# The moving weights of the q, k and v sums read column by column from two runs of 256 columns

## The chip, the cores and the metric

The kernel runs on one core of a Trainium2 chip. The metric is the time of one execution on the device, in microseconds. The kernel before takes 2652.43 us, the median of three runs (2650.87 to 2653.06).

## What is computed

The reference is a trunk of two layers over 256 tokens of width 2048, in float32. A layer is a mixer (two attentions side by side, with gates) and a gated feed-forward part with a convolution. What the change touches is the first step of the mixer: the products of the normalised input with the columns of `w_in` that give queries, keys and values.

```python
h = rmsnorm(x, norm_mix[l]) * (1.0 + sc_a) + sh_a
qa, ka, va, qb, kb, vb, ga, gb = split_cols(h @ w_in[l])
qa = rotary_partial(rmsnorm(qa.reshape(B, S, HA, HEAD_DIM), qn_a[l]), pos)
ka = rotary_partial(rmsnorm(ka.reshape(B, S, GA, HEAD_DIM), kn_a[l]), pos)
va = va.reshape(B, S, GA, HEAD_DIM)
ya = window_attention(qa, ka, va, sink_a[l]) @ w_proj_a[l]
qb = rmsnorm(qb.reshape(B, S, HB, HEAD_DIM), qn_b[l])
kb = rmsnorm(kb.reshape(B, S, HB, HEAD_DIM), kn_b[l])
vb = vb.reshape(B, S, HB, HEAD_DIM)
yb = neighbourhood_attention(qb, kb, vb, rel_bias_b[l]) @ w_proj_b[l]
```

The columns of q, k and v number 4608, in nine groups of 512; a head has 128 of them.

## The kernel before

**Numbers.** Every large product runs in a reduced float32 form. An operand is kept as two halves, a rounded high part and what is left of it, and a product is the sum of three matmuls: high by high, high by low, low by high. Weights come from memory in units of 16 blocks of 128 by 128 (tile `w`, 1 MB each) in the order of use. ScalarE rounds a unit (L346) and VectorE subtracts to get the low half (L347), into tiles `hl` that hold the high and the low half of eight blocks each, 1024 columns per half.

**Two ways round.** In most products the weights are stationary and 256 tokens are the moving operand; that is `feature_block`, L363 to L365, with the tile `ps`. In the sums for q, k and v it is the other way: `tokens` (L417 to L434) keeps 128 tokens of the input `h` stationary and moves four blocks of weights, 512 neighbouring columns of `hl`, past it, so that tokens lie on partitions of the result. Each call has two PSUM tiles `ps_t` of 512 columns, one for each half of the tokens, and for every chunk `kc` of the input six matmuls, L427 to L429 for each half. There are 1728 of them in all.

**Stages.** Layer 0 goes over its nine groups three times, each time with as many of the 16 chunks as are normalised by then (`K_ENDS`): the first part leaves its sums in the packs in SBUF through copies on ScalarE (L967), the second and third add to them on VectorE (L969). Layer 1 has one part with all 16 chunks, and its readers work on PSUM directly: copies of v on ScalarE (L980), and in `qk_rows` a square per head and token half on ScalarE (L599, tile `qsq`) and the product with the root on VectorE (L609, tile `qn`). In layer 0 those two read the packs. Group 0 holds k and v of the first attention, 256 columns each; groups 4 and 7 are v of the second; the others are four heads of q or k.

**Order.** The program's order is set by the loops; background jobs (the products for the modulation on VectorE at L246, attention heads, copies of 32 by 32 blocks on GpSimd) are handed out once per unit of 16 blocks by `tick`. Weights are split a unit or two ahead. PSUM has four buffers for sums, so that a call's readers work while the next call's matmuls run.

Of the kernel before, what the change touches and what calls it, by code (L numbers as in the profile page):

```python
# [11 lines left out]
AF = mybir.ActivationFunctionType  # L12
ALU = mybir.AluOpType
AX = mybir.AxisListType

P = 128
# [4 lines left out]
HEAD = 128  # L21
HA, GA, HB = 8, 2, 8
# [121 lines left out]
def encoder(ctx: ExitStack, tc: tile.TileContext, a: dict, out: bass.AP):  # L144
    nc = tc.nc
# [46 lines left out]
    def place(tag, n, dt, name):  # L192
        return sp.tile([P, n, S], dt, name=name, tag=tag)
# [113 lines left out]
    def later(n, fn):  # L307

        if n == 0:
            fn()  # L310
        else:
            bg.defer(lambda: later(n - 1, fn))
# [54 lines left out]
    class Stream:  # L367
# [49 lines left out]
        def tokens(self, h, kcs):  # L417

            pss = [mm.tile([P, 512], F32, name=f"ps{self.l}_{self.u}_t{t}", tag="mm") for t in range(2)]
            for kc in kcs:  # L420
                for _ in range(4):
                    hl, j = self.next_block()
                j -= 3
                hi, lo = hl[:, 0, j * P : (j + 4) * P], hl[:, 1, j * P : (j + 4) * P]
                for t, ps in enumerate(pss):
                    xh, xl = (h[kc][:, i, t * P : (t + 1) * P] for i in range(2))
                    nc.tensor.matmul(ps[:], xh, hi, start=kc == kcs[0], stop=False)  # L427
                    nc.tensor.matmul(ps[:], xh, lo, start=False, stop=False)  # L428
                    nc.tensor.matmul(ps[:], xl, hi, start=False, stop=kc == kcs[-1])  # L429
                if self.l == 0 and self.u == 1 and self.at == 4:  # L430
                    warm(WARM_ROW)
                if self.at == UB:
                    self.tick()
            return pss  # L434

    def split(dst, src, scale=None, held=False):

# [152 lines left out]

    def qk_rows(pss, heads, rot, gain, dst, then, moved=False, pinned=False):

        cols = 0
        n = heads * HEAD
        ss = sm.tile([P, 8], F32, name="qss", tag="qss")
        for t, ps in enumerate(pss):
            for i in range(heads):
                sq = at.tile([P, HEAD], F32, name="qsq", tag="qsq", bufs=1)
                nc.scalar.activation(  # L599
                    out=sq[:], in_=ps[:, cols + i * HEAD : cols + (i + 1) * HEAD], func=AF.Square,  # L600
                    accum_out=ss[:, t * heads + i : t * heads + i + 1],
                )
        rs = sm.tile([P, 8], F32, name="qrs", tag="qrs")
        rsqrt(rs[:, : 2 * heads], ss[:, : 2 * heads], HEAD, 2 * heads)
        def norm():
            qn = at.tile([P, 8 * HEAD], F32, name="qn", tag="qn", bufs=1)[:, : 2 * n]
            qn = qn.rearrange("p (t h d) -> p t h d", t=2, d=HEAD)
            for t, ps in enumerate(pss):
                product = nc.vector.tensor_tensor(  # L609
                    out=qn[:, t],  # L610
                    in0=ps[:, cols : cols + n].rearrange("p (h d) -> p h d", d=HEAD),
                    in1=rs[:, t * heads : (t + 1) * heads].unsqueeze(2).broadcast_to([P, heads, HEAD]),
                    op=ALU.mult,
                )
                if pinned:
                    tc.keep_in_program_order(product)
            if rot is not None:
                x1, x2 = qn[:, :, :, :HALF], qn[:, :, :, HALF:ROT]
                tab = [rot[:, i].unsqueeze(2).broadcast_to([P, 2, heads, HALF]) for i in range(4)]
                tm = []  # L620
                for i in range(2):
                    z = ev.tile([P, S], F32, name=f"rt{i}", tag="z")
                    z = z[:].rearrange("p (i t h d) -> p i t h d", i=2, t=2, h=4)
                    tm += [z[:, 0, :, :heads], z[:, 1, :, :heads]]
                for i, src in enumerate((x1, x2, x2, x1)):
                    nc.vector.tensor_tensor(out=tm[i], in0=src, in1=tab[i], op=ALU.mult)
                nc.vector.tensor_tensor(out=x1, in0=tm[0], in1=tm[1], op=ALU.subtract)
                nc.vector.tensor_tensor(out=x2, in0=tm[2], in1=tm[3], op=ALU.add)
            bg.defer(lambda: turn(qn))

        def turn(qn):
            if moved:
                nc.vector.transpose(out=qn, in_=qn)
                moved_blocks(dst.rearrange("p h (t s) -> p h t s", t=2), qn.rearrange("p t h d -> p h t d"))

                def scaled():
                    tc.keep_in_program_order(nc.scalar.activation(out=dst, in_=dst, func=AF.Identity, scale=gain))
                    then()

                later(QK_STEPS, scaled)  # L640
                return
            for t in range(2):
                ps = ax.tile([P, 4, P], F32, name="qtp", tag="ax")
                for h in range(heads):
                    nc.tensor.transpose(ps[:, h], qn[:, t, h], ident[:])
                scaled = nc.scalar.activation(
                    out=dst[:, :, t * P : (t + 1) * P], in_=ps[:, :heads], func=AF.Identity, scale=gain
                )
                if pinned:
                    tc.keep_in_program_order(scaled)  # L650
            then()

        bg.defer(lambda: bg.defer(lambda: bg.defer(norm)))
# [116 lines left out]
    with tc.high_priority():  # L770
# [13 lines left out]
        for i in range(KC // 4):  # L784
            sq = place(("y0", "y1", "y2", "a")[i], 12 if i == 3 else 4, F32, f"sq_in{i}")
# [16 lines left out]
        ps = ax.tile([P, 2], F32, name="ss_in", tag="ss", bufs=1)  # L802
# [34 lines left out]
    for l in range(L):  # L837
        st = Stream(l) if l == 0 else nxt
        mod = mods.get(l)
        if l == 0:  # L840
            h = led("h0_0", K_ENDS[0][0][1])
# [13 lines left out]
        if l:  # L855
# [13 lines left out]
            h = bare.h  # L869
# [6 lines left out]
        ready, heads = [0], [0]  # L876
# [78 lines left out]
        for pi, (groups, gates) in enumerate(parts):  # L955
            last = pi == len(parts) - 1
            for g, part in enumerate(groups):
                have_h(part)
                pss = st.tokens(h, part)
                if pi == max(0, len(parts) - 2) and g == 0:  # L960
                    gains, sink, cw, rots = small(l)
                dst = packs[g // 3][:, 4 * (g % 3) : 4 * (g % 3) + 4]
                rows = dst.rearrange("p (t a) s -> p t (a s)", t=2)
                if not last or pi > 0:
                    for t, ps in enumerate(pss):
                        if pi == 0:
                            nc.scalar.copy(rows[:, t], ps[:])  # L967
                        else:
                            nc.vector.tensor_tensor(out=rows[:, t], in0=ps[:], in1=rows[:, t], op=ALU.add)  # L969
                    pss = [rows[:, t] for t in range(2)]  # L970
                if not last:
                    continue

                def turned(g=g):
                    ready[0] = g + 1

                vcol = {0: GA * HEAD, 4: 0, 7: 0}.get(g)
                if vcol is not None and pi == 0:
                    for t in range(2):
                        nc.scalar.copy(rows[:, t, vcol:], pss[t][:, vcol:])  # L980
                if g == 0:
                    qk_rows(pss, GA, rots[1], gains[:, 1:2], kTa, turned, g in MOVED_QK[l], l == 1)
                elif g < 3:
                    qk_rows(pss, 4, rots[0], gains[:, 0:1], dst, turned, g in MOVED_QK[l], l == 1)
                elif vcol is None:
                    qk_rows(pss, 4, None, gains[:, 3:4] if g in (3, 6) else gains[:, 2:3], dst, turned, g in MOVED_QK[l], l == 1)
                else:
                    turned()
                if g == (1 if l in EARLY else 2):
                    bg.add(job, ATT[l])  # L990


            have_h(gates)
            for mo in range(BARE[0] if l else 0, KC):

                def gate_a(ps):
                    src = ps
                    if pi > 0:
                        nc.vector.tensor_tensor(out=ya[:, mo], in0=ps, in1=ya[:, mo], op=ALU.add)  # L999
                        src = ya[:, mo]  # L1000
                    if last:
                        half_tanh(ya[:, mo], src)
                    elif pi == 0:
                        nc.scalar.copy(ya[:, mo], ps)

                st.features([hs[k] for k in gates], [gate_a])
# [14 lines left out]
        for tag in ("y0", "y1", "y2"):  # L1021
            t = place(tag, 4, F32, f"gb{l}_{tag}")
            gb += [t[:, i] for i in range(4)]
        for i in range(2):
            t = paired(F32, f"gb{l}_{i}")
# [207 lines left out]
```

## Time and profile before

| | |
|---|---|
| median of three runs | 2652.43 us |
| span of the profiled execution | 2649.9 us, on one core |
| instructions in the trace | 50997 |
| memory read | 695.06 MB, 263 GB/s over the span |
| reads of the weight units | 463 of 1024 KB, 4.9 us each from issue to landing |

The span runs from the first to the last instruction of the profiled execution; its own time isn't given apart from it, and 2.5 us lie between the span and the median. In the lines of groups, a name such as `ps_t<-hl,h` gives the tile written and the tiles read; then come the shapes, the count, the busy time in us and the mean duration of one in ns, and the idle time just before them. A matmul's record lasts from its start to the end of its last result, and records of matmuls that follow each other overlap. In the view of waits, a row gives the total in us, how often, and the longest.

### The profile page before, as it was taken

What the parts mean: (1) busy time and instruction counts of PE and PEld (TensorE: products, weight loads), DVE (VectorE), ACT (ScalarE), POOL (GpSimd) and SP (SyncE); (2) the same over time, 40 slices, a digit from 0 to 9 for tenths busy, and PEclk for the clock granted to TensorE, in tenths of its full rate; (3) what the DMA queues carried; (4) which work ended last, traced back from release to release, by engine and by line L of the source; (5) the groups of instructions that cost most, each with busy time, mean ns of one, the idle gap of its engine ahead of it and who ended that gap; (6) DMA issues with size and microseconds to landing.
All of it is one profiled execution on the core that took longest, in us unless ns stands there. A gap on an engine that the chain in (4) does not pass through costs nothing.

```text
span 2649.9 us, 50997 instructions
## 1 busy us (share of the span) xinstructions
PE 2638.7 (100%) x21164; PEld 2553.2 (96%) x21164; DVE 2121.3 (80%) x2979; ACT 1407.4 (53%) x2280; POOL 235.7 (9%) x345
## 2 busy tenths in 40 slices
PE   9999999999999999999999999999999999999999
PEld 7888899999999999999998889999999999999999
DVE  8898998997987888788886778868888876655664
ACT  5445865456653554355554666555575445544553
POOL 0001100000000000000002558620000000000000
PEclk9999999999999999999999999999999999999999
DMA  9988789885777877777766666677757775555554
GB/s 366 344 332 300 264 299 353 325 305 210 281 293 284 298 290 295 291 287 291 297 226 239 252 223 244 251 266 273 275 183 273 287 271 192 193 197 195 195 191 143
DMA packets 102185, 700.45 MB, mean 264 GB/s; under 512 B 12865, under 2 KB 15169, under 8 KB 18113
## 3 DMA queue, kind: packets, MB, share of 16 engines
q1 hardware_dynamic: 101954, 697.20, 71.4%
q8 instruction: 165, 2.70, 0.4%
q14 instruction: 66, 0.54, 0.1%
HBM read 695.06 MB, written 2.10 MB: 263 GB/s over the span
## 4 chain that ended last, share of the span: by engine, by line
PE 90%; DVE 6%; ACT 1%; issue 1%; DMA 1%; POOL 0%; DVEq 0%; ACTq 0%
PE ps L363 25%; PE ps L365 25%; PE ps L364 25%; PE ps_t L429 4%; PE ps_t L428 4%; PE ps_t L427 4%; DVE hl L347 2%; DVE aw L246 2%; PE sc L674 1%; DMA aw<-in_aw 1%; PE po L712 1%; ACT hl L346 1%; PE warm L462 0%; PE tp L704 0%; PE cb L776 0%
## 5 line engine op out<-in xcount | busy, mean ns | idle before, releaser
L347 DVE TENSOR_TENSOR hl<-w,hl 128x1024 fp32r<-128x1024 f32 x928 | 1132.7, 1226 | 341.6 <-ACT hl L346 337.1
L346 ACT CAST hl<-w 128x1024 fp32r<-128x1024 f32 x928 | 970.5, 1049 | 752.1 <-PE ps L365 522.7
L363 PE MATMUL ps<-h,hl 128*128 128x256 f32 x3328 | 922.1, 277 | 1.3 <-DVE ya L999 0.6
L364 PE MATMUL ps<-h,hl 128*128 128x256 f32 x3328 | 919.2, 276 | 0.0
L365 PE MATMUL ps<-h,hl 128*128 128x256 f32 x3328 | 919.0, 276 | 0.0
L363 PEld LDWEIGHTS ps<-h,hl 128*128 128x128 f32 x3328 | 624.6, 188 | 2.3 <-DVE ya L999 0.8
L364 PEld LDWEIGHTS ps<-h,hl 128*128 128x128 f32 x3328 | 624.7, 188 | 0.4 <-DVE h L522 0.2
L365 PEld LDWEIGHTS ps<-h,hl 128*128 128x128 f32 x3328 | 624.2, 188 | 0.0
L246 DVE CUSTOM_DVE_ANT_0 aw<-aw,cact,ab 128x2048 f32<-128x2048 f32 x189 | 443.7, 2348 | 9.1 <-DMA aw<-in_aw 8.9
L428 PE MATMUL ps_t<-hl,h 128*128 128x512 f32 x576 | 225.1, 391 | 0.4
L427 PE MATMUL ps_t<-hl,h 128*128 128x512 f32 x576 | 223.2, 392 | 2.2 <-ACT h L521 1.6
L429 PE MATMUL ps_t<-hl,h 128*128 128x512 f32 x576 | 224.5, 391 | 0.0
L1078 DVE SCALAR_TENSOR_TENSOR u<-ps,cw,u 128x255 f32<-128x255 f32 x304 | 146.4, 481 | 94.4 <-ACT u L1076 90.0
L1076 ACT ACTIVATE u<-ps,cw 128x256 f32<-128x256 f32 x152 | 85.7, 564 | 216.5 <-PE ps L365 216.5
L365 PE MATMUL ps<-merged,hl 128*128 128x256 f32 x512 | 141.7, 277 | 0.2
L364 PE MATMUL ps<-merged,hl 128*128 128x256 f32 x512 | 141.5, 276 | 0.0
L363 PE MATMUL ps<-merged,hl 128*128 128x256 f32 x512 | 141.5, 277 | 0.0
L364 PE MATMUL ps<-act_o,hl 128*128 128x256 f32 x512 | 141.3, 276 | 0.0
L365 PE MATMUL ps<-act_o,hl 128*128 128x256 f32 x512 | 141.3, 276 | 0.0
L363 PE MATMUL ps<-act_o,hl 128*128 128x256 f32 x512 | 141.0, 276 | 0.0
L427 PEld LDWEIGHTS ps_t<-hl,h 128*128 128x128 f32 x576 | 107.9, 188 | 25.8 <-ACT h L521 2.7
L428 PEld LDWEIGHTS ps_t<-hl,h 128*128 128x128 f32 x576 | 108.1, 188 | 24.3 <-DVE hl L347 2.1
(244 smaller groups left out, 4807.1 us busy)
## 6 DMA issues: line engine op xcount, KB each, us to landing
w<-in_ws SPq DMA_DIRECT2D x463, 1024.0 KB, 4.9
aw<-in_aw SPq DMA_DIRECT2D x189, 1024.0 KB, 5.1
p<-in_bias SPq DMA_DIRECT2D x16, 256.0 KB, 4.5
x<-in_xT SPq DMA_DIRECT2D x4, 512.0 KB, 5.3
aw_o<-in_aw SPq DMA_DIRECT2D x2, 1024.0 KB, 12.2
out<-x SPq DMA_DIRECT2D x16, 128.0 KB, 1.9
w<-in_ws SPq DMA_DIRECT2D x2, 512.0 KB, 11.5
aw_b<-in_aw SPq DMA_DIRECT2D x1, 1024.0 KB, 18.2
```

The source lines that it names most:

```text
L246: product = nc.vector.tensor_tensor_reduce(out=raw[:], in0=raw[:], in1=cact[:], scale=1.0, scalar=ab[:, i : i + 1], op0=ALU.mult, op1=ALU. ...
L346: nc.scalar.copy(hl[:, 0], r)
L347: nc.vector.tensor_tensor(out=hl[:, 1], in0=r, in1=hl[:, 0].bitcast(F32), op=ALU.subtract)
L363: nc.tensor.matmul(out, hi, act[0], start=first, stop=False)
L364: nc.tensor.matmul(ps[:, :S], hi, act[1], start=False, stop=False)
L365: nc.tensor.matmul(out, lo, act[0], start=False, stop=last)
L427: nc.tensor.matmul(ps[:], xh, hi, start=kc == kcs[0], stop=False)
L428: nc.tensor.matmul(ps[:], xh, lo, start=False, stop=False)
L429: nc.tensor.matmul(ps[:], xl, hi, start=False, stop=kc == kcs[-1])
L674: nc.tensor.matmul(sc[:, t], q[i][:, t * P : (t + 1) * P], k[j], start=i + j == 0, stop=(i, j) == by(q)[-1])
L1076: nc.scalar.activation(out=u, in_=ps, func=AF.Identity, scale=w[:, 1:2], bias=w[:, 3:4])
L1078: nc.vector.scalar_tensor_tensor(out=u[:, to], in0=ps[:, of], scalar=w[:, j : j + 1], in1=u[:, to], op0=ALU.mult, op1=ALU.add)
```

## The change

The moving operand of the three matmuls, `hi` or `lo`, is the same 512 columns, read as column 0 of the first 256, column 0 of the second 256, column 1 of the first, column 1 of the second, and so on: two runs, 1024 bytes apart, in turn. PSUM is written in 512 neighbouring columns as before, so column 2s + a of `ps_t` now holds what was column 256a + s. `tokens` gives its callers a view of PSUM that undoes this, `[tokens, a, s]`, and all readers of `ps_t` (126 instructions) go through it: they step over every second word. In the packs the columns lie as before, and the other operands and results keep their patterns. On every engine the built program has the same instructions in the same order as before; only line numbers behind L593 are one lower.

```diff
                 j -= 3
-                hi, lo = hl[:, 0, j * P : (j + 4) * P], hl[:, 1, j * P : (j + 4) * P]
+                hi, lo = (hl[:, i, j * P : (j + 4) * P].rearrange("p (a s) -> p s a", a=2) for i in range(2))
                 for t, ps in enumerate(pss):
...
-            return pss
+            return [ps[:].rearrange("p (s a) -> p a s", a=2) for ps in pss]
...
     def qk_rows(pss, heads, rot, gain, dst, then, moved=False, pinned=False):
 
-        cols = 0
         n = heads * HEAD
...
-                    out=sq[:], in_=ps[:, cols + i * HEAD : cols + (i + 1) * HEAD], func=AF.Square,
+                    out=sq[:], in_=ps[:, i // 2, i % 2 * HEAD : i % 2 * HEAD + HEAD], func=AF.Square,
...
-                    out=qn[:, t],
-                    in0=ps[:, cols : cols + n].rearrange("p (h d) -> p h d", d=HEAD),
-                    in1=rs[:, t * heads : (t + 1) * heads].unsqueeze(2).broadcast_to([P, heads, HEAD]),
+                    out=qn[:, t].rearrange("p (a h) d -> p a h d", h=2),
+                    in0=ps[:, : heads // 2].rearrange("p a (h d) -> p a h d", d=HEAD),
+                    in1=rs[:, t * heads : (t + 1) * heads].rearrange("p (a h) -> p a h", h=2).unsqueeze(3).broadcast_to([P, heads // 2, 2, HEAD]),
...
-                rows = dst.rearrange("p (t a) s -> p t (a s)", t=2)
+                rows = dst.rearrange("p (t a) s -> p t a s", t=2)
                 if not last or pi > 0:
                     for t, ps in enumerate(pss):
                         if pi == 0:
-                            nc.scalar.copy(rows[:, t], ps[:])
+                            nc.scalar.copy(rows[:, t], ps)
                         else:
-                            nc.vector.tensor_tensor(out=rows[:, t], in0=ps[:], in1=rows[:, t], op=ALU.add)
+                            nc.vector.tensor_tensor(out=rows[:, t], in0=ps, in1=rows[:, t], op=ALU.add)
...
-                vcol = {0: GA * HEAD, 4: 0, 7: 0}.get(g)
+                vcol = {0: 1, 4: 0, 7: 0}.get(g)
```

## The prediction, made before the changed kernel ran

> **What bounds the kernel now.** The page's busy lines, its slices and its chain come first.
>
> ```profile
> span 2649.9 us, 50997 instructions
> PE 2638.7 (100%) x21164; PEld 2553.2 (96%) x21164; DVE 2121.3 (80%) x2979; ACT 1407.4 (53%) x2280; POOL 235.7 (9%) x345
> ...
> PEclk9999999999999999999999999999999999999999
> ...
> PE 90%; DVE 6%; ACT 1%; issue 1%; DMA 1%; POOL 0%; DVEq 0%; ACTq 0%
> PE ps L363 25%; PE ps L365 25%; PE ps L364 25%; PE ps_t L429 4%; PE ps_t L428 4%; PE ps_t L427 4%; DVE hl L347 2%; DVE aw L246 2%; PE sc L674 1%; DMA aw<-in_aw 1%; PE po L712 1%; ACT hl L346 1%; PE warm L462 0%; PE tp L704 0%; PE cb L776 0%
> ```
>
> TensorE is busy for 2638.7 of 2649.9 us at a full granted clock in every slice, and 90% of the chain that ended last is matmuls. The three lines that the change rewrites (tile ps_t, L427 to L429) hold some 12% of that chain. Who makes TensorE wait is asked next, in the view of waits for that engine alone.
>
> ```profile
> PE cb L776 <- DMA cact<-in_c: 2.6, 1, 2.6
> PE ps_t L427 <- ACT h L521: 1.6, 3, 1.0
> PE sc L674 <- ACT packB L646: 0.7, 1, 0.7
> PE ps L363 <- DVE ya L999: 0.6, 1, 0.6
> PE ps_t L427 <- ACT hl L346: 0.5, 1, 0.5
> ```
>
> All waits together are under 7 us. So TensorE has no slack into which a slower matmul could sink: what a matmul gains or loses is gained or lost by the kernel, nearly one for one. The four stretches in which the sums for q, k and v run (the three parts of layer 0, and layer 1) show the same, in the view by windows (columns: length, then busy us and instructions of PE, PEld, DVE, ACT, POOL, then clock and DMA):
>
> ```profile
> 19.70:66.20 46.50, 44.35 (x202) 34.81 (x203) 42.63 (x46) 25.69 (x36) 0.00 (x0) 1.00 0.95 373
> 101.00:178.00 77.00, 77.00 (x340) 63.28 (x339) 72.00 (x90) 31.34 (x35) 0.00 (x0) 1.00 0.94 344
> 216.00:309.50 93.50, 93.26 (x442) 76.98 (x441) 86.41 (x141) 62.64 (x162) 18.16 (x6) 1.00 0.80 289
> 1393.00:1601.50 208.50, 207.76 (x961) 172.97 (x960) 151.31 (x218) 122.71 (x254) 101.99 (x160) 1.00 0.64 238
> ```
>
> PE is full in each, but for 2 us of the first. VectorE (DVE) comes near: 72.00 of 77.00 us. The same windows in the view by lines tell how many of the PE instructions are these sums; one of the three lines in each, in the windows' order:
>
> ```profile
> L428 PE MATMUL ps_t<-hl,h 128*128 128x512 f32 x56 | 22.1, 400 | 0.4
> L428 PE MATMUL ps_t<-hl,h 128*128 128x512 f32 x112 | 43.8, 391 | 0.0
> L427 PE MATMUL ps_t<-hl,h 128*128 128x512 f32 x120 | 47.3, 394 | 0.0
> L428 PE MATMUL ps_t<-hl,h 128*128 128x512 f32 x288 | 112.3, 390 | 0.0
> ```
>
> Three times each: 168, 336, 360 and 864 matmuls, 1728 in all.
>
> **What one of these matmuls costs now.** The groups, then the timeline of TensorE in layer 1 and, for comparison, in a stretch of 256-column matmuls:
>
> ```profile
> L428 PE MATMUL ps_t<-hl,h 128*128 128x512 f32 x576 | 225.1, 391 | 0.4
> L427 PE MATMUL ps_t<-hl,h 128*128 128x512 f32 x576 | 223.2, 392 | 2.2 <-ACT h L521 1.6
> L429 PE MATMUL ps_t<-hl,h 128*128 128x512 f32 x576 | 224.5, 391 | 0.0
> ```
>
> ```profile
> 1499.70 0.39 PE L428 MATMUL ps_t<-hl,h 128*128 128x512 f32 x1
> ...
> 1502.65 0.39 PE L429 MATMUL ps_t<-hl,h 128*128 128x512 f32 x1
> ```
>
> ```profile
> 399.80 0.28 PE L363 MATMUL ps<-h,hl 128*128 128x256 f32 x1
> ...
> 401.97 0.28 PE L364 MATMUL ps<-h,hl 128*128 128x256 f32 x1
> ```
>
> The 391 ns of a record is a lifetime; records overlap. The cost is from start to start: from 1499.70 to 1502.65 lie 13 steps, 2.95 us, so 227 ns for 512 columns. The short ones take 19 steps in 2.17 us, 114 ns for 256 columns. Half the columns take half the time, so there is no fixed part to speak of: both are **0.443 ns for each column** of the moving operand. All 1728 matmuls then hold 1728 x 0.227 = 392 us. That a matmul's time is its columns and nothing else is why the order in which columns are fetched could matter: the stream of columns is the thing that is full.
>
> **The change, part by part.** It adds no instruction, removes none and moves none; every engine issues the same sequence, and no DMA differs. Two access patterns change.
>
> *The moving operand.* Before, 512 neighbouring words per partition; now words 0, 256, 1, 257 and so on: no two columns in a row are neighbours. No row of this trace has a moving operand read that way, so its price is bounded by rows around it. From below: no price, 227 ns; and a gain, if all that the windows hold above 227 ns for these matmuls and 114 for each other PE instruction should go. That is 46.5 - 168 x 0.227 - 34 x 0.114 = 4.5 us in the first, 0.2, 2.5 and 1.3 us in the others, 9 us in all. From above, the slowest rows that stream columns:
>
> ```profile
> 272.96 1.03 PE L674 MATMUL sc<-packA 128*128 128x256 f32 x4
> 273.64 0.58 PE L427 MATMUL ps_t<-hl,h 128*128 128x512 f32 x1
> ```
>
> ```profile
> 2.58 7.16 PE L776 MATMUL cb<-cact,one 1*128 1x512 f32 x8 [2.58 <-DMA cact<-in_c]
> ```
>
> Two plain f32 matmuls of 256 columns (four records) take 0.68 us until the next one starts, 1.33 ns per column, three times what the reduced form takes. The eight records of 512 columns at the start take 7.16 us, 895 ns each, nearly four times. So the ends are 227 and 895 ns, or +0 and +668 x 1728 = +1154 us. I take twice the present cost, 454 ns: it is what comes out if a fetch now brings in two neighbouring columns and each column will need a fetch of its own. It is nearest to the matmul's own row, and the 0.68 us row lies as far above it as 227 lies below. **+227 ns x 1728 = +392 us.**
>
> [...]
>
> *The readers.* 126 instructions now take every second word of PSUM:
>
> ```profile
> L969 DVE TENSOR_TENSOR packB<-ps_t,packB x24: 673/686/692, 132.6 to 310.0; 128x512 f32<-128x512 f32 x24
> L969 DVE TENSOR_TENSOR packA<-ps_t,packA x12: 681/684/694, 107.4 to 252.6; 128x512 f32<-128x512 f32 x12
> L967 ACT COPY packB<-ps_t x12: 574/587/594, 38.9 to 66.3; 128x512 f32<-128x512 f32 x12
> L599 ACT ACTIVATE qsq<-ps_t x52: 255/277/302, 1414.6 to 1605.5; 128x128 f32<-128x128 f32 x52
> ```
>
> ```profile
> L347 DVE TENSOR_TENSOR hl<-w,hl 128x1024 fp32r<-128x1024 f32 x928 | 1132.7, 1226 | 341.6 <-ACT hl L346 337.1
> ```
>
> Bounds again: nothing, or as much as twice the elements. On VectorE 512 more elements cost 1226 - 685 = 541 ns (L347 against L969). The view by windows of L969 alone has 17 of these adds in each of two stretches:
>
> ```profile
> 101.00:178.00 77.00, 11.61 (x17) 1.00 0.94 344
> 216.00:309.50 93.50, 10.64 (x17) 1.00 0.80 289
> ```
>
> That would be 9 us more in each, against 5 us that VectorE has to spare in the one stretch and 7 in the other. So if the matmuls cost nothing more, VectorE would be late by 4 + 2 = 6 us at most; if they take 454 ns, the former grows by 336 x 0.227 = 76 us and the readers lie beside it. I take nothing for them. ScalarE has a third or more of every window free.
>
> *What else moves.* The stages grow, so splits of weights, the ada products and GpSimd's block moves get more room; but TensorE waits for them under 7 us today, so at most that returns. Stages without these sums keep their time.
>
> **Sum.** The profiled execution, 2649.9 us of span with 2.5 us to the median of 2652.4, grows by 392 us: 2652.4 + 392 = **3044 us**. Within this case, 430 to 490 ns per matmul, 3003 to 3107 us.
>
> **Rivals.**
>
> *Four turns a column.* If a fetch now brings in four neighbouring columns and the feed of 1.77 ns per four (4 x 0.443) is the time of one fetch, each column costs 1.77 ns, a matmul 907 ns, and the kernel 2652 + 680 x 1.728 = 3827 us. For it: the feed has no fixed part and is full now, so one fetch per column is the plain reading; the 895 ns row shows that the engine can be that slow. Against it: nothing here shows how many columns a fetch holds. Chance 0.20. [...]
>
> *A part of the price, or one between.* Fetches overlap, so that the stream costs more but not a whole multiple: 2660 to 3000 us, or 3110 to 3600 us, as with the 0.68 us row (680 ns, +453 x 1.728 = 783 us, 3435 us). Chance 0.14.
>
> *Nothing.* Both runs are held at once: of two streams that go forward in step, each fetch serves its own run's next columns, and the matmul stays at 227 ns. Then only readers can show, 0 to +6 us: 2650 to 2659 us. For it: the pattern is just two runs, not scattered. The point from which it decides: the feed must keep two fetched pieces, not one. [...] Chance of within 0.2% of before: 0.12.
>
> *Faster.* The other side, by one mechanism in the token sums: two runs in turn take away what holds a step above its floor. What the windows offer is the 9 us above: 2643 us. It needs the two runs to be fetched independently, and a price below zero from the first column. [...] Chance of over 0.2% faster: 0.12.
>
> *That the change doesn't do what it says* is excluded by its text: the pattern of all 1728 is rewritten in one line.
>
> **How the numbers follow.** Twice the cost 0.42, four times 0.20, other prices 0.14, nothing 0.12, faster 0.12. This kernel's measurement tells some 0.2% (5 us) from no change. Slower is 0.42 + 0.20 + 0.14 = 0.76. The likeliest case's own range is 3003 to 3107. Leaving out either end would drop over 2 in 10 (four turns and part of the prices between; nothing and faster), so the range runs from 2640 to 3830.
>
> **What would show it.** Steps from start to start on L427 to L429: 227 ns says no price, 454 the forecast, 907 the rival. The 256-column matmuls should stay at 114 ns. The four windows should grow with their counts (by 38, 76, 82 and 196 us) with PE still full; a VectorE that is full in 101 to 178 with matmuls at 227 ns says readers. The rows of L969, L967 and L599 show the readers' price directly: 685, 587 and 277 ns before. The prediction is wrong if the feed keeps both runs at hand, and far too low if a fetch is worth four columns.

## The result, and the profile after

The changed kernel takes 2642.46 us (median of six runs, 2641.43 to 2643.28) against 2650.97 us for the kernel before (six runs): a ratio of 0.9965, 95% interval 0.9953 to 0.9976. It is 8.5 us faster. The forecast was 3044 us.

The page of the changed kernel, its busy lines and its chain (lines behind L593 are one lower than before):

```profile
span 2640.7 us, 51000 instructions
PE 2619.6 (99%) x21164; PEld 2555.7 (97%) x21164; DVE 2120.1 (80%) x2979; ACT 1405.9 (53%) x2280; POOL 247.6 (9%) x345
...
PE 85%; DVE 6%; DMA 3%; POOL 3%; ACT 2%; issue 2%; SPq 0%; POOLq 0%; DVEq 0%; ACTq 0%
```

TensorE's share of the chain fell from 90% to 85%, GpSimd's rose from 0 to 3% and the DMAs' from 1 to 3%: something that TensorE used to hide now shows. First the matmuls themselves. Two rows of TensorE's timeline in layer 1, and the three groups of the sums:

```profile
1499.52 0.38 PE L427 MATMUL ps_t<-hl,h 128*128 128x512 f32 x1
...
1502.97 0.38 PE L428 MATMUL ps_t<-hl,h 128*128 128x512 f32 x1
```

```profile
L427 PE MATMUL ps_t<-hl,h 128*128 128x512 f32 x576 | 217.4, 382 | 4.3 <-ACT h L521 2.7
L428 PE MATMUL ps_t<-hl,h 128*128 128x512 f32 x576 | 219.6, 382 | 1.1 <-DVE hl L347 0.9
L429 PE MATMUL ps_t<-hl,h 128*128 128x512 f32 x576 | 218.6, 380 | 0.0
```

From 1499.52 to 1502.97 lie 16 steps: 216 ns each, not 227 and not 454. 1728 x 11 ns = 19 us should be gone. The idle column tells of the rest: 5.4 us before these lines where there were 2.6. The view of waits for TensorE names the others:

```profile
PE sc L673 <- ACT packB L645: 4.3, 1, 4.3
PE tp L703 <- ACT p L692: 3.8, 4, 2.7
PE ps_t L427 <- ACT h L521: 2.7, 3, 1.1
PE cb L775 <- DMA cact<-in_c: 2.5, 1, 2.5
PE ps_t L427 <- ACT hl L346: 1.5, 1, 1.5
```

Two waits have grown, from 0.7 to 4.3 and from 0.2 to 3.8 us. The second of them in the trace before:

```profile
PE tp L704 <- ACT p L693: 0.2, 1, 0.2
```

The same engine order in both kernels allows a finer reading: each of these matmuls has its counterpart in the other trace. How far the changed kernel is ahead, worked out from the starts of the same matmul in both traces:

```
start in the trace before, us      ahead by, us
  19.7   first sum of layer 0        0.8
  66.1   end of its first part       0.9
 106.5 ... 172.4  second part        1.0 ... 4.6   (1.1 to 1.2 for every 96 sums)
 221.7 ... 281.1  third part         5.0 ... 7.9
 284.6                               5.4
 317.1   after layer 0's sums        5.6
1393.0   first sum of layer 1        5.2
1551.9                              12.6
1555.4                               7.1
1602.4   after layer 1's sums        9.2
2584.7                               9.2
```

So every stretch of sums wins what 11 ns a step makes, and it is given back at three places: all of it in layer 0's first part (waits for h and hl), 2.5 us at once in the third, 5.5 us at once in layer 1. In the third part TensorE waits 2.7 us for ScalarE (`p`, L692), but ScalarE had itself stood 3.67 us for VectorE's `nm` (L681), and VectorE has hardly a pause from 258 to 277 us (18.97 of 19.00 us busy). Its `nm` starts at 271.81 us, before at 277.06: 5.25 us ahead, which is the lead that TensorE is left with there. The last of the three in the trace after, TensorE first:

```profile
1539.24 0.38 PE L427 MATMUL ps_t<-hl,h 128*128 128x512 f32 x1
1543.90 1.65 PE L673 MATMUL sc<-kA,qA 128*128 128x256 f32 x6 [4.28 <-ACT packB L645]
1545.35 0.63 PE L428 MATMUL ps_t<-hl,h 128*128 128x512 f32 x1
1545.77 0.63 PE L429 MATMUL ps_t<-hl,h 128*128 128x512 f32 x1
```

```profile
1541.00:1542.00 1.00, 0.00 (x0) 0.00 (x0) 0.84 (x2) 0.97 (x4) 0.36 (x2) 0.86 1.01 426
1542.00:1548.50 6.50, 4.60 (x14) 3.97 (x15) 4.88 (x11) 5.96 (x21) 6.00 (x13) 0.50 0.91 349
```

TensorE stands for 4.28 us, and then its steps take 420 ns: from 1542 to 1548.5 us the granted clock is 0.50, and 4.6 us of that is work. The clock was 1.00 from 1541 to 1541.5 us, so the mean of 0.86 over the first window puts the fall near 1541.7 us, 2.1 us after the last matmul's record ended at 1539.62. This wait cost more than its length: by an estimate from these rows, 4.6 us at half speed lose 2.3 us, beside the 3.6 us by which the wait grew. Followed back, ScalarE's packB stands in its queue behind an exponential that waits for VectorE, and VectorE's product stands for the roots from GpSimd, whose queue is full of block copies. ScalarE, VectorE and GpSimd in the trace after, then GpSimd in the trace before:

```profile
1536.28 0.51 ACT L684 ACTIVATE p<-p,nm 128x256 f32<-128x256 f32 x1 [5.58 <-DVE nm L681]
```

```profile
1530.13 1.29 DVE L608 TENSOR_TENSOR qn<-ps_t,qrs 128x512 f32<-128x512 f32 x2 [6.50 <-POOL qrs L493]
```

```profile
1508.45 12.02 POOL L318 COPY p<-packA 32x128 f32<-32x128 f32 x16 [4.71 <-DVE packA L324]
1521.28 7.10 POOL L318 COPY p<-packA 32x128 f32<-32x128 f32 x16 [0.81 <-DVE packA L324]
1528.46 1.64 POOL L493 TENSOR_TENSOR qrs<-qss,mhalf 128x8 f32<-128x8 f32 x1
```

```profile
1515.94 7.27 POOL L318 COPY p<-packA 32x128 f32<-32x128 f32 x16 [10.49 <-DVE packA L324]
1530.23 7.28 POOL L318 COPY p<-packA 32x128 f32<-32x128 f32 x16 [7.02 <-DVE packA L324]
1537.59 1.63 POOL L493 TENSOR_TENSOR qrs<-qss,mhalf 128x8 f32<-128x8 f32 x1
```

Before, GpSimd idled 7 to 10 us ahead of each batch; after, 0.8 to 5 us, and one batch took 12.02 us instead of 7.27. The trace tells where the batch was slow. Seven of its 16 copies met no instruction of VectorE and took 288 ns each; six began while VectorE was at a subtraction (L347) or at a product for the modulation (L246), took 1.2 to 2.3 us, and ended some 0.15 us after that instruction. The longest, and the product beside it:

```profile
1513.39 2.25 POOL L318 COPY p<-packA 32x128 f32<-32x128 f32 x1
```

```profile
1513.12 2.37 DVE L246 CUSTOM_DVE_ANT_0 aw<-aw,cact,ab 128x2048 f32<-128x2048 f32 x1
```

In the batch of the trace before, two copies met such an instruction at their start. So in this order GpSimd's copies fell beside more of VectorE's work; that the one holds up the other is read from these times, and no run tests it.

The readers, last, in the view by tile of ps_t:

```profile
L968 DVE TENSOR_TENSOR packA<-ps_t,packA x12: 675/682/692, 106.4 to 247.0; 128x512 f32<-128x512 f32 x12
L966 ACT COPY packB<-ps_t x12: 570/588/594, 38.2 to 65.3; 128x512 f32<-128x512 f32 x12
L598 ACT ACTIVATE qsq<-ps_t x52: 256/277/299, 1408.3 to 1596.4; 128x128 f32<-128x128 f32 x52
```

682, 588 and 277 ns where there were 684, 587 and 277: every second word of PSUM cost ScalarE and VectorE nothing here.

### The profile page after: what moved, and what is told of

Its sections match the earlier page's. It is cut to its first block, busy times and chain, and to the rows that moved or that the text cites. A ratio compares the mean times of both kernels' runs of the same rounds, so it can differ in the third digit from the quotient of the medians.

```text
span 2640.7 us, 51000 instructions
## 1 busy us (share of the span) xinstructions
PE 2619.6 (99%) x21164; PEld 2555.7 (97%) x21164; DVE 2120.1 (80%) x2979; ACT 1405.9 (53%) x2280; POOL 247.6 (9%) x345
## 4 chain that ended last, share of the span: by engine, by line
PE 85%; DVE 6%; DMA 3%; POOL 3%; ACT 2%; issue 2%; SPq 0%; POOLq 0%; DVEq 0%; ACTq 0%
PE ps L363 26%; PE ps L365 25%; PE ps L364 25%; PE ps_t L428 2%; PE ps_t L427 2%; PE ps_t L429 2%; DVE hl L347 2%; DMA aw<-in_aw 2%; DVE aw L246 2%; POOL packA L318 1%; POOL p L318 1%; DMA w<-in_ws 1%; ACT hl L346 1%; PE sc L673 1%; PE po L711 1%
## 5 line engine op out<-in xcount | busy, mean ns | idle before, releaser
L347 DVE TENSOR_TENSOR hl<-w,hl 128x1024 fp32r<-128x1024 f32 x928 | 1132.6, 1226 | 325.2 <-ACT hl L346 321.2
L246 DVE CUSTOM_DVE_ANT_0 aw<-aw,cact,ab 128x2048 f32<-128x2048 f32 x189 | 443.7, 2348 | 12.3 <-DMA aw<-in_aw 12.2
L427 PE MATMUL ps_t<-hl,h 128*128 128x512 f32 x576 | 217.4, 382 | 4.3 <-ACT h L521 2.7
L428 PE MATMUL ps_t<-hl,h 128*128 128x512 f32 x576 | 219.6, 382 | 1.1 <-DVE hl L347 0.9
L429 PE MATMUL ps_t<-hl,h 128*128 128x512 f32 x576 | 218.6, 380 | 0.0
```

Source lines behind the costliest of these rows:

```text
L246: product = nc.vector.tensor_tensor_reduce(out=raw[:], in0=raw[:], in1=cact[:], scale=1.0, scalar=ab[:, i : i + 1], op0=ALU.mult, op1=ALU. ...
L347: nc.vector.tensor_tensor(out=hl[:, 1], in0=r, in1=hl[:, 0].bitcast(F32), op=ALU.subtract)
```

## Experiments

### What a moving operand costs, pattern by pattern

Three small kernels hold matmuls in the same reduced form, each pattern 120 or 160 times with weights loaded anew.

```diff
+    ("rowA", 0, [[1, 512]]),
+    ("twoA", 0, [[1, 256], [256, 2]]),
+    ("pairs", 0, [[2, 128], [256, 2], [1, 2]]),
+    ("four", 0, [[1, 128], [128, 4]]),
+    ("stepTwo", 0, [[2, 512]]),
...
+        moving = bass.AP(tensor=view.tensor, offset=view.offset, ap=[view.ap[0]] + steps)
+        for i in range(N):
+            tc.keep_in_program_order(
+                nc.tensor.matmul(ps[:, :n], sta[:, i % 4 * P : (i % 4 + 1) * P], moving, start=True, stop=True)
+            )
```

> Nothing of the trunk is computed: 160 matmuls each of 26 patterns of the moving operand, one after the other, with the weights loaded anew for each, in the kernel's reduced float32 form; steps from start to start are read. Theory A, the loss sits where a single run goes on from one 64-byte piece to the next (one turn in 17: 213 ns becomes 227), and a second run in turn hides it: 512 neighbours 227 ns, two runs column by column 216 whatever their distance, pairs and quads in turn 216, sixteens in turn 227, four and eight runs 216, short rows of 256 neighbours 113.5 and two runs of 128 109. Theory B, it is no matter of runs but of where the moving words lie against the stationary ones: then the four rows at offsets 0, 16, 32 and 48 columns differ by 10 ns or more, one of them is at 216, and two runs differ among their offsets as much. Theory C, my prediction's: a fetch brings two neighbours; it holds for scattered words if not for two runs: steps of two or four columns in one run, and 32 runs, take 430 to 450 ns.

The groups by line; busy time less the length of one, over 159, is the step from start to start:

```profile
L69 PE MATMUL eight<-mov,sta 128*128 128x512 f32 x160 | 78.1, 667 | 0.0
L69 PE MATMUL stepTwo<-mov,sta 128*128 128x512 f32 x160 | 72.4, 629 | 0.0
L69 PE MATMUL pairs<-mov,sta 128*128 128x512 f32 x160 | 53.5, 502 | 0.0
L69 PE MATMUL four<-mov,sta 128*128 128x512 f32 x160 | 45.5, 448 | 0.0
L69 PE MATMUL rowD<-mov,sta 128*128 128x512 f32 x160 | 37.5, 395 | 0.0
L69 PE MATMUL rowA<-mov,sta 128*128 128x512 f32 x160 | 36.4, 389 | 0.0
L69 PE MATMUL twoFar<-mov,sta 128*128 128x512 f32 x160 | 34.7, 379 | 0.0
L69 PE MATMUL twoD<-mov,sta 128*128 128x512 f32 x160 | 34.7, 379 | 0.0
L69 PE MATMUL twoA<-mov,sta 128*128 128x512 f32 x160 | 34.7, 379 | 0.0
L69 PE MATMUL shortRow<-mov,sta 128*128 128x256 f32 x160 | 19.4, 283 | 0.0
L69 PE MATMUL shortTwo<-mov,sta 128*128 128x256 f32 x160 | 18.0, 275 | 0.0
```

(34.7 - 0.38) / 159 = 216 ns for two runs, whatever their distance and wherever they start. A single row takes 226.5 at the offset 0 and 233 at the offset of 48 columns: it depends on where it starts, and two runs do not. (The weights lay where they were for all patterns, so whether it is the place against the weights that counts isn't shown.) A step of two words, 451 ns, shows that the price of my forecast exists, but for other patterns. Theory A is right on two runs and wrong on the rest: pairs in turn (333), quads (250), four runs (283) and eight (487) should have been as good as two; no run shows its pieces of 64 bytes. Of theory B a spread of 7 ns among the four rows is left, where 10 or more and one row at 216 were expected. Theory C holds, nearly to its numbers, for steps and for 32 runs (431 to 460).

What the fast and the slow patterns have in common suggested a new theory: TensorE might read even and odd places of the stream separately. In a single row a reader of even places would see words 0, 2, 4; with two runs in turn it would see one run, 0, 1, 2. The next kernel tests that.

> Nothing of the trunk is computed: patterns of the moving operand again, 160 matmuls each, and 12 copies and subtractions of 256 columns whose results are written straight (flatA) or into two runs in turn (foldA). Theory A, TensorE's stream has two readers, one for columns at even places and one for those at odd places, each with a little store of its own, and is held up when a reader needs a new piece for (nearly) every column or two: overlapping runs (0, 1, 1, 2, 2, 3), one run read twice and two runs from an odd start all step at 216 ns; two runs with a step of two words inside give each reader what a single row gives it, 226 to 233; with a step of four or eight words, 430 to 460; six runs, three for each reader, 430 to 490 as with eight. Rival B, one store for both, that keeps the last pieces of any run: six runs lie between four (283) and eight (487) and two runs with a step of two stay at 216. Writing into two runs in turn: no price, as reading every second word had none, or at most 0.7 ns a column, 170 ns.

```profile
L59 PE MATMUL twoStepFour<-mov,sta 128*128 128x512 f32 x160 | 72.7, 632 | 0.0
L59 PE MATMUL six<-mov,sta 128*128 128x510 f32 x160 | 47.6, 463 | 0.0
L59 PE MATMUL row<-mov,sta 128*128 128x512 f32 x160 | 36.4, 389 | 0.0
L59 PE MATMUL twoStepTwo<-mov,sta 128*128 128x512 f32 x160 | 36.5, 389 | 0.0
L59 PE MATMUL same<-mov,sta 128*128 128x512 f32 x160 | 34.7, 379 | 0.0
L59 PE MATMUL overlap<-mov,sta 128*128 128x512 f32 x160 | 34.7, 379 | 0.0
L74 ACT CAST foldA<-x 128x256 fp32r<-128x256 f32 x12 | 8.3, 693 | 0.0
L71 ACT CAST flatA<-x 128x256 fp32r<-128x256 f32 x12 | 5.5, 455 | 0.0
L75 DVE TENSOR_TENSOR foldA<-x,foldA 128x256 fp32r<-128x256 f32 x12 | 7.4, 618 | 0.1
L72 DVE TENSOR_TENSOR flatA<-x,flatA 128x256 fp32r<-128x256 f32 x12 | 4.9, 408 | 8.0 <-ACT flatA L71 8.0
```

Two runs with a step of two words inside would give each reader what a row gives it, and they cost what a row costs: 227 ns. With a step of four words: 453. One run read twice, and runs that overlap: 216. So theory A has it. Six runs fell out of it: 297 ns, where 430 to 490 were expected of three runs for each reader. Writing into two runs costs ScalarE 238 ns on 256 columns (693 against 455), and VectorE, which also reads one operand in that order, 210 ns (618 against 408): both more than the most I allowed.

> Nothing of the trunk is computed: 120 matmuls each of patterns with more than one run, at other distances in words between the runs (two256w: two runs, 256 words apart). Open since e5: six runs took 297 ns, eight 487. Theory A, a reader keeps two pieces, and runs 256 bytes (64 words) or a multiple apart hinder each other beside that: four runs (two per reader) fall from 283 towards 216 to 230 at distances that are no multiple of 64 words (132, 136, 144), pairs in turn from 333 towards 227 likewise, eight runs from 487 to under 350. Theory B, a reader keeps one piece and the distance is of no matter: four stay at 280 to 290, pairs at 330, eight at 430 to 490 whatever the distance. Two runs stay at 216 in both.

```profile
L69 PE MATMUL pairs264w<-mov,sta 128*128 128x512 f32 x120 | 39.4, 496 | 0.0
L69 PE MATMUL four144w<-mov,sta 128*128 128x512 f32 x120 | 32.7, 438 | 0.0
```

Over 119 steps each, four runs 271 to 283 ns, pairs 327 to 328, six 287 to 292, eight 433 to 487, two 216 at every distance. So distance matters little; 64 words between eight runs and multiples of 64 between four are the worst, by 12 to 53 ns. Theory B is nearer, with six runs against it, which lie close to four and not to eight: whether there are readers that keep pieces, and how many, stays open.

### Where the gain went

Layer 0 alone, and layer 1 alone, have the new order:

```diff
-                hi, lo = (hl[:, i, j * P : (j + 4) * P].rearrange("p (a s) -> p s a", a=2) for i in range(2))
+                hi, lo = (hl[:, i, j * P : (j + 4) * P] for i in range(2))
+                if self.l == 0:
+                    hi, lo = (v.rearrange("p (a s) -> p s a", a=2) for v in (hi, lo))
```

> Two runs in turn in layer 0 alone, layer 1 as before. If the gain is local and what is lost is lost to waits in the same layer, as the two traces put side by side say (5 us ahead at the end of layer 0's sums, 9 after layer 1's), this is 2645.5 to 2647 us against 2651. Rival, that the layers' gains hang together (layer 1 starts earlier against the loads): 2649 or more.

> Two runs in turn in layer 1 alone, layer 0 as before. Local gains: 864 steps of 11 ns less the 5.8 us given back there, 2646.5 to 2648 us, with the wait of TensorE for the turned q (ACT packB) of 4 us again. Rival, the wait comes from layer 0's earlier end and is not there: 2641.5 us.

Layer 0 alone: 2647.09 us, ratio 0.9986 (0.9977 to 0.9995). Layer 1 alone: 2646.89 us, ratio 0.9984 (0.9976 to 0.9993). That is 4.3 and 4.5 us against the 2651.43 of the kernel before on the same chip, 8.8 together, where both at once give 8.5: within intervals of 2 to 3 us on either side, the layers don't touch each other. (Layer 0 alone lies 0.1 us above what was expected, and under the rival's 2649.) Layer 1 alone has the wait again:

```profile
PE sc L675 <- ACT packB L647: 4.3, 1, 4.3
```

Then layer 1's chain of waits is cut at GpSimd, and the same edit is made to the kernel before as a control:

```diff
-MOVED = [(0,0), (8,8)]
+MOVED = [(0,0), (0,8)]
```

> The changed kernel, but the first attention's probabilities of layer 1 are turned by TensorE (32 transposes) instead of by VectorE and GpSimd's block copies. If layer 1's loss is GpSimd being late with the roots for the next q behind its copies, VectorE's wait for qrs and TensorE's wait for packB of 4.3 us go, with the slow steps behind it; the transposes cost 32 x 0.11 = 3.5 us and some switching: 2639 to 2642 us, and before layer 1's transposes the lead over the kernel before passes 13 us. Rival, the wait has another cause (ScalarE's own queue): it stays, and the transposes come on top: 2645 to 2648 us.

> The kernel before with the first attention's probabilities of layer 1 turned by TensorE, the control of e4. If layer 1's wait of 4.3 us is made by the faster steps, there is nothing to win here and the 32 transposes cost: 2653 to 2655.5 us. Rival, that edit is simply better by itself: 2648.5 to 2649.5, as much under the kernel before as e4 is under the changed one.

On the changed kernel 2639.91 us (0.9957, 0.9945 to 0.9970, of the kernel before): 2.5 us less than without the edit, though this interval and that of the changed kernel overlap. On the kernel before 2653.82 us (1.0010, 1.0001 to 1.0019): 2.4 us more, just clear of none. The wait for packB is no longer among TensorE's waits, and VectorE's wait for the roots in layer 1 is 4.4 us in place of 10.9. So the transposes cost about 2.4 us, and the lateness of this chain cost the changed kernel about 5 us that the kernel before didn't pay, with 1 or 2 us of doubt on each. The edit takes 128 copies from GpSimd and 8 instructions from VectorE at once, so it doesn't part the two. One number was missed: the lead stood at 10.2 us by 1504 us and not over 13, as transposes start before the point at which the wait was.

### The same order for the other matmuls

If two runs cost 112 ns for 256 columns in place of 113.5 to 120, the other products can have it too. Tokens are kept even ones first; the moving operand reads both halves in turn, so PSUM comes out in the order of tokens, and readers write back to the kept order.

```diff
-        out = ps[:, : act[0].shape[-1]]
+        out = ps[:, : act[0].shape[1] * act[0].shape[2]]
...
+def in_turn(v):
+    return v.rearrange("p (a s) -> p s a", a=2)
...
-                    feature_block(ps, hl, j, (act[:, 0], act[:, 1]) if not isinstance(act, tuple) else act,
+                    feature_block(ps, hl, j, (in_turn(act[:, 0]), in_turn(act[:, 1])) if not isinstance(act, tuple) else act,
...
-                gated(ya[:, mo], ya[:, mo], ps)
+                gated(runs(ya[:, mo]), runs(ya[:, mo]), runs_of(ps))
...
-                split(act_of(c), u[:, 1])
+                split(act_of(c), u[:, 1], turned=True)
```

> All of the trunk is computed: the changed kernel, and also the other large products move their 256 tokens in two runs of 128 in turn; tokens are kept even ones first, readers of PSUM undo the order, the gated halves of the feed-forward part are written into two runs. 18816 short matmuls step at 112 ns in place of 114.3 on average: 2.5 x 18816 = 47 us less if it goes through as it stands, 2595; as with the sums a part is given back where VectorE or ScalarE come last: 2595 to 2620. Rival: the readers in three dimensions and the folded writes cost VectorE so much that it bounds the feed-forward part: 2640 or more.

> The kernel of e6 with the first attention's probabilities of layer 1 turned by TensorE, as in e4. There that took 2.5 us off: 2 to 3 us under e6 if layer 1's wait is the same, level with it if the wait went with the faster steps.

2603.02 us for the first (0.9816, 0.9803 to 0.9829, of the kernel before) and 2600.07 us for the second (0.9807, 0.9793 to 0.9820). The first is 39 us under the changed kernel. Its steps, worked out from the starts of neighbouring short matmuls, are 111.7 ns on average in place of 114.2, which makes the 47 us that were expected of them; a part is given back in longer waits, among them 3.0 us in which TensorE waits for VectorE's low halves of weights (0.5 in the changed kernel). The second has the lowest median here, 51 us under the kernel before; that it is 3 us under the first agrees with what was expected, but the single runs of the two overlap. The folded writes cost VectorE what the small kernel said, and most of it is hidden; one group in the first of the two, which took 418 ns in the changed kernel:

```profile
L459 DVE TENSOR_TENSOR act_o<-u,act_o 128x256 fp32r<-128x256 f32 x32 | 19.9, 623 | 2.0 <-ACT act_o L458 2.0
```

## Why the prediction was wrong

**The step that failed** is the price of the moving operand: "I take twice the present cost, 454 ns: it is what comes out if a fetch now brings in two neighbouring columns and each column will need a fetch of its own." The runs show 216 ns. The premise under it, that neighbours in the stream must be neighbours in memory for a fetch to serve both, is what is wrong: in the new order they never are, and the matmul got faster. What a fetch brings in, no run shows. Several patterns fit a model of mine: two readers take places in turn, and the time goes by how far apart the words lie that one of them takes one after the other. Four words apart, 451 ns (one run with a step of two) and 453 (two runs with a step of four); two words apart, 227 (a row, and two runs with a step of two); neighbours, 216 (two runs). The two readers are a model that fits these patterns, not a thing seen. It doesn't explain four, six and eight runs (283, 297 and 487 ns), or pairs and quads in turn (333 and 250): for pairs the model has 451 ns if a reader keeps one run at hand, and 227 if it keeps two. So that the order of the columns made the gain is shown; by what mechanism stays open.

**What was read rightly and used wrongly.** 0.443 ns a column at both lengths did show a time that goes by the columns, 227 and 114 ns; that a feed was full was my estimate from it. I took most other orders to be worse. If it is full, that leaves room as well for an order that gains, and I bounded the gain by what the windows held above 227 ns, as if 227 were a floor. The upper end was misread too: the 895 ns row was taken at 2.6 to 9.7 us, and the kernel's warm-up matmuls of one shape last 421 ns before 13 us and 275 ns after 17.4, so it is hardly a price at full speed.

**The rivals.** "Faster", with a chance of 0.12 and 2643 us, gave the side, and the time by luck: its condition, two runs fetched independently, was not shown, and its 9 us were to come from the excess over 227, while 19 came from 227 itself, of which over half was given back. The measured time lies inside the stated range only because this rival was let into it. "Four turns" had 907 ns a matmul; the dearest pattern of the small kernels, eight runs, took 487. "Nothing" foresaw that two runs cost no more than the row's 227 ns, not that they cost less.

**One for one.** "What a matmul gains or loses is gained or lost by the kernel, nearly one for one" was wrong for a gain: 19 us won, 8.5 kept. The view of waits showed under 7 us, but it tells of slack that TensorE lacks, not of how little slack the others have behind it. With steps 5% shorter, GpSimd's queue in layer 1 and VectorE's, by way of ScalarE, in layer 0's third part came last. For layer 1 this is shown by cutting the chain, with its control, as far as the noise allows; for the 2.5 us of layer 0's third part and the 2 us of its first it is read from the trace alone.

**The readers** cost nothing, as taken: where VectorE came late, it wasn't by them.

## What to carry to other kernels

On TensorE in this reduced float32 form, a moving operand of neighbouring words is not the fastest: two runs, column by column, took 5% less (216 ns against 227), did not depend on where they started but for an odd word (217), and cost the readers of PSUM nothing (588 and 682 ns against 587 and 684). Four or more runs, pairs in turn, or a step inside a single run cost from a fifth more to a little over twice as much (271 to 487 ns), so the pattern is to be measured before it is built in. And where one engine hides all others, look before speeding it up at which queue has the least idle time behind it: over half of this gain was given back where another queue came late, and a wait of 4.28 us left the next 4.6 us of work at a granted clock of 0.50.

## What the runs showed of the hardware that was not expected

- A row of 512 neighbours takes 227 to 233 ns by its offset, 237 from an odd word; two runs 216 at all six starts and distances of the first small kernel and at the four distances of the third, 217 from an odd word.
- One run read twice (0, 0, 1, 1) takes 216 ns too, so the gain is not that of two places in memory.
- Reading every second word of PSUM cost ScalarE and VectorE nothing (588 and 682 ns for 512 columns, 587 and 684 for neighbours); writing into two runs of SBUF in turn cost ScalarE 693 in place of 455 ns, and VectorE, which also read one operand so, 618 in place of 408.
- In a wait of 4.28 us the granted clock fell to 0.50 some 2.1 us in and stayed there until about 1548.5 us, and steps of 216 ns took 420 to 430.
- Copies on GpSimd that took 288 ns alone took up to 2.25 us where VectorE was at a long subtraction or product.
